# FFN activations: reciprocal rms, their combinations and a second copy of the high parts in PSUM; GpSimd splits none of the second half

## Chip, cores and metric

The kernel runs on one core of one Trainium2 chip. The metric is the device time of one execution in microseconds (us). TensorE (PE in the profile) multiplies, with weight loads shown as PEld; VectorE is DVE, ScalarE is ACT, GpSimd is POOL, and SyncE (SP) issues the DMAs. PSUM holds eight banks of 128 x 512 float32; SBUF holds all else on the core.

## What is computed

A hybrid decoder layer in float32 over 1024 tokens of width 1024: RWKV-7 time mixing beside dilated attention, then cross-attention to a memory, then the squared-ReLU MLP that the change is about, then a final norm. Cut to what matters:

```
D_MODEL = 1024; SEQ = 1024; FFN_DIM = 4096
def rmsnorm(x, g):
    return x * rsqrt(mean(x * x, axis=-1, keepdims=True) + 1e-6) * g
...
        h = h + memory_cross_attention(...)
        u = rmsnorm(h, norm_ffn_g[l]) @ ffn_w1[l]
        h = h + jnp.square(jax.nn.relu(u)) @ ffn_w2[l]
    return rmsnorm(h, norm_final_g)
```

## The kernel before

Activations lie transposed: `hT[d][half]` is a 128 x 512 tile of 128 channels (d = 0 to 7) by one half of the tokens. A float32 product is made of three matmuls on a high and a low part: `split(hi, lo, src)` rounds `src` to the high part with a ScalarE copy (line 128) and subtracts it from `src` for the low part (line 129), on VectorE or, where the caller says so, on GpSimd. PE then multiplies high by high, high by low and low by high (lines 1419 to 1421 in the MLP). Weights are split in the same way: ScalarE makes `wh` (line 1381), GpSimd `wl` (line 1382).

The MLP multiplies 2 x 2 blocks with seven block products in place of eight. Each of 16 up items (1024 x 256 of `ffn_w1`) and 16 down items (`ffn_w2`) runs seven products j = 0 to 6, each of 4 x 3 matmuls of 128 x 512 into one `ms` bank (`seventh`). Product j needs four split tiles `com[j]` of the activations and one split sum of weights. `up_evac` and `down_evac` take the products out of PSUM on VectorE; `up_evac` also makes the seven combinations of squared ReLUs and writes them to DRAM (`uscr`).

Where the activations come from:

- For the up items `first_coms(half)` makes them. `rms` turns the sums of squares into the reciprocal rms, spreads it over 128 x 512 by a matmul into PSUM (`pr`, from the pool `fps`), and copies it to SBUF (`rs`, line 1148). `normed` multiplies a tile of `hT` by its gain and by `rs` (line 1545). Half 0 gives `com[0]` and `com[1]`. Half 1 gives `com[3]`, `com[4]`, `com[2]`, `com[5]`, `com[6]` in that order, four tiles each: `normed`, an addition or subtraction (lines 1569, 1576, 1581, 1586), a split. Of its 20 splits GpSimd makes 12 low parts, VectorE 8.
- For the down items `second(g, j)` loads four tiles `ur` from `uscr` and splits them with VectorE. This is a *fill*: 28 tiles for each of four groups g of down items. Six SBUF buffers hold `ur` (tags `nt` four times, `rs`, `ssq`), so a load waits on SP's queue until an earlier tile has been split.

The first three up items run j = 0 and 1 early (`prologue`), while half 1 is being made; then item 0 runs j = 3, 4, 2, and products 5 and 6 after it, so it asks for all five groups of half 1 within a few products. After that the item order is 0, (5 of the item before), 1, (6 of the item before), 2, 3, 4. In a fill the same order asks for 28 tiles in eleven products.

What sets the order on each engine: the code is written in the order above, and a scheduler at build time orders each engine's instructions by its own estimate of times, within what the data and the buffers allow. On the chip each engine then runs its list strictly in that order. `acc_tile` gives one of two PSUM banks (`pacc`, two buffers) which the products before the MLP use; the MLP doesn't touch them.

Of the kernel before, what the change touches and what calls it, by code (L numbers as in the profile page):

```python
# [9 lines left out]
F32 = mybir.dt.float32  # L10
F32R = mybir.dt.float32r
AF = mybir.ActivationFunctionType
ALU = mybir.AluOpType
# [4 lines left out]
P = 128  # L18
D = 1024
S = 1024  # L20
H2 = 512
# [20 lines left out]
def hybrid_layer(ctx, tc, x, mem, norm_mix_g, w_in, shift_mu, w0, w2, a0, a2, g2, k_k, k_a, r_k, gn_w, gn_b,  # L42
                 p_rwkv, p_attn, w_out, norm_x_g, norm_mem_g, xa_wq, xa_wkv, xa_wo, norm_ffn_g, ffn_w1, ffn_w2,
                 norm_final_g, out):
    nc = tc.nc
# [4 lines left out]
    def nm(s):  # L50
        cnt[0] += 1
        return f"{s}_{cnt[0]}"
# [71 lines left out]
    def mm(ps, lhsT, rhs, start=True, stop=True):  # L124
        return nc.tensor.matmul(ps, lhsT, rhs, start=start, stop=stop)  # L125

    def split(hi, lo, src, lo_eng=None):
        nc.scalar.copy(hi, src)  # L128
        (lo_eng or nc.vector).tensor_tensor(lo, src, hi.bitcast(F32), op=ALU.subtract)  # L129
# [43 lines left out]
    def acc_tile():  # L173
        return pacc.tile([P, H2], F32, tag="acc", name=nm("acc"))
# [955 lines left out]
            nc.scalar.activation(sq, h, AF.Square)  # L1130
            nc.vector.tensor_tensor(ssq, ssq, sq, op=ALU.add)

    def rms(ssq, got, ps_tile):

        ps = ps_tile()
        for j in range(4):
            mm(ps[:, j:j + 1], ssq[:, j * P:(j + 1) * P], ones[:, 0:1])
        rt = bt.tile([P, 4], F32, tag="rt", name=nm("rt"), bufs=2)
        nc.scalar.activation(rt, ps[:, 0:4], AF.Sqrt, bias=eps_n, scale=1.0 / D)
        nc.vector.reciprocal(rt, rt)  # L1140
        rs = bt.tile([P, H2], F32, tag="rs", name=nm("rs"), bufs=1)
        for j in range(4):
            nc.vector.tensor_scalar_mul(rs[:, j * P:(j + 1) * P], ident, rt[:, j:j + 1])
        yield
        pr = ps_tile()
        for j in range(4):
            mm(pr[:, j * P:(j + 1) * P], ones, rs[:, j * P:(j + 1) * P])
        nc.scalar.copy(rs, pr)
        got.append(rs)
        yield  # L1150

    def norm_gen(ssq, res, half, gcol, ring):
        got = []
        yield from rms(ssq, got, ms_tile)
        rs = got[0]
        for d in range(NK):
            t = bt.tile([P, H2], F32, tag="nt", name=nm("nt"))
            nc.vector.scalar_tensor_tensor(t, hT[d][half], vec[:, gcol + d:gcol + d + 1], rs, op0=ALU.mult,
                                           op1=ALU.mult)
            ph = act_pair(ring)  # L1160
            split(ph[0], ph[1], t, nc.gpsimd if d % 2 else nc.vector)
            res.append(ph)
            yield
# [48 lines left out]
    ssqs, n1 = [None, None], [[], []]  # L1212
# [145 lines left out]
    fps = ctx.enter_context(tc.tile_pool(name="fps", bufs=2, space=PSUM, reuse_waits="tile"))  # L1358
    rings["U"] = fs
    RING = "BBACCAU"  # L1360
    com = [None] * 7

    def staged():
        return fs.tile([P, H2], F32, tag="sg", name=nm("sg"), bufs=7)

    def com_tiles(j):
        if RING[j] == "U":
            return [tuple(fs.tile([P, H2], F32R, tag=t, name=nm("u"), bufs=4) for t in ("uh", "ul")) for _ in range(4)]
        return [act_pair(RING[j]) for _ in range(4)]
# [155 lines left out]
    def down_views(g, q):  # L1525
        v = ffn_w2[0][g * D:(g + 1) * D, :].rearrange("(k h r) c -> h r k c", h=2, r=P)
        return [v[h, :, :, (2 * q + e) * P:(2 * q + e + 1) * P] for e in range(2) for h in range(2)]

    def second(g, j):

        com[j] = com_tiles(j)
        for i, ph in enumerate(com[j]):
            t = bt.tile([P, H2], F32, tag=UR[un[0] % 6], name=nm("ur"), bufs=4 if UR[un[0] % 6] == "nt" else 1)
            un[0] += 1
            r0 = ((g * 4 + i) * 7 + j) * P
            nc.sync.dma_start(t, uscr[r0:r0 + P, :])
            split(*ph, t, nc.vector)

    def first_coms(half):

        got = []
        yield from rms(ssqs[half], got, lambda: fps.tile([P, H2], F32, tag="f", name=nm("fm")))

        def normed(t, d):
            nc.vector.scalar_tensor_tensor(t, hT[d][half], vec[:, V_GFFN + d:V_GFFN + d + 1], got[0], op0=ALU.mult,
                                           op1=ALU.mult)

        if half == 0:
            for e in range(2):
                com[e] = com_tiles(e)  # L1550
                made.append(e)
                for i in range(4):
                    t = fs.tile([P, H2], F32, tag=("uh", "ul")[e], name=nm("b"), bufs=4)
                    normed(t, i + 4 * e)
                    split(*com[e][i], t, nc.gpsimd if i % 2 else nc.vector)
                    if e:

                        nc.vector.tensor_tensor(t, t, b0[0][i], op=ALU.subtract)
                    b0[e].append(t)
                    yield  # L1560
            return
        for j in range(2, 6):
            com[j] = com_tiles(j)
        b12 = []
        for i in range(4):
            b12.append(staged())
            normed(b12[i], i)
            t = staged()
            nc.vector.tensor_tensor(t, b12[i], b0[0][i], op=ALU.subtract)
            split(*com[3][i], t, nc.vector if i == 2 else nc.gpsimd)  # L1570
            yield
        made.append(3)
        for i in range(4):
            t = staged()
            normed(t, i + 4)
            nc.vector.tensor_tensor(b12[i], t, b12[i], op=ALU.subtract)
            split(*com[4][i], b12[i], nc.vector if i == 2 else nc.gpsimd)
            yield
        made.append(4)
        for i in range(4):  # L1580
            nc.vector.tensor_tensor(b0[0][i], b12[i], b0[0][i], op=ALU.add)
            split(*com[2][i], b0[0][i], nc.gpsimd if i % 2 else nc.vector)
            yield
        made.append(2)
        for i in range(4):
            nc.vector.tensor_tensor(b0[1][i], b0[1][i], b12[i], op=ALU.subtract)
            split(*com[5][i], b0[1][i], nc.gpsimd if i % 2 else nc.vector)
            yield
        made.append(5)
        com[6] = com_tiles(6)  # L1590
        for i in range(4):
            b22 = staged()
            normed(b22, i + 4)
            split(*com[6][i], b22, nc.gpsimd if i % 2 else nc.vector)
            yield
        made.append(6)

    UR, un = ("nt", "nt", "rs", "nt", "nt", "ssq"), [0]
    b0, made = [[], []], []

    def run(it, j):
        if it.get("fill"):
            second(it["fill"][0], j)
        while j not in made:
            next(coms, None)
        yield from seventh(it["st"], j, it["w"](j))
        it["st"].setdefault("seen", []).append(j)
        it["evac"](it["st"], j)
        yield
# [10 lines left out]
    def prologue():  # L1620
        for p in range(PRO):
# [3 lines left out]
            yield from run(it, 1)  # L1625

    weave((xout(o1, 1), 64, 0, 100), (first_coms(0), 10, 0, 80))

    def finish(d, half):
# [48 lines left out]
    def stream():  # L1678
        prev, ready = None, []
        for it, whole in items():  # L1680
# [22 lines left out]
            prev = it  # L1703

    coms = first_coms(1)
    weave((chain(prologue(), stream()), 48, 0, 100), (coms, 22, 0, 90))
_INS = ['x', 'mem', 'norm_mix_g', 'w_in', 'shift_mu', 'w0', 'w2', 'a0', 'a2', 'g2', 'k_k', 'k_a', 'r_k', 'gn_w', 'gn_b',
# [20 lines left out]
```

## Time and profile before

| what | us |
|---|---|
| median of 3 runs | 2441.41 (2440.43 to 2444.42) |
| the profiled execution, its own time | 2439.77 |
| its span, first to last instruction | 2438.1 |
| PE busy in the span | 2304.0 (95%) |
| VectorE busy | 1589.6 (65%) |
| ScalarE busy | 1046.3 (43%) |
| GpSimd busy | 922.5 (38%) |
| mean granted TensorE clock | 0.983 |

The MLP takes the span from 1723 us (the first matmul of line 1419) to its end at 2438 us. To read a stretch, compare its count of matmuls with that of a stretch where PE never waits: PE's busy time covers overlapping matmuls and is no measure by itself. A granted clock of 1.00 is 2.4 GHz, the lower of the two levels is 1.2 GHz.

### The profile page before, as it was taken

What the parts mean: (1) busy time and instruction counts of PE and PEld (TensorE: products, weight loads), DVE (VectorE), ACT (ScalarE), POOL (GpSimd) and SP (SyncE); (2) the same over time, 40 slices, a digit from 0 to 9 for tenths busy, and PEclk for the clock granted to TensorE, in tenths of its full rate; (3) what the DMA queues carried; (4) which work ended last, traced back from release to release, by engine and by line L of the source; (5) the groups of instructions that cost most, each with busy time, mean ns of one, the idle gap of its engine ahead of it and who ended that gap; (6) DMA issues with size and microseconds to landing.
All of it is one profiled execution on the core that took longest, in us unless ns stands there. A gap on an engine that the chain in (4) does not pass through costs nothing. (4 is left out here: it accounts for less than half of the span.)

```text
span 2438.1 us, 46897 instructions
## 1 busy us (share of the span) xinstructions
PE 2304.0 (95%) x18645; PEld 1834.2 (75%) x18645; DVE 1589.6 (65%) x2723; ACT 1046.3 (43%) x2032; POOL 922.5 (38%) x749
## 2 busy tenths in 40 slices
PE   6999999999999999999999999999889999899997
PEld 5777777777777777777678888887668887677775
DVE  6638677686786612232555664456799999797785
ACT  5525645645456434334433454444422223344344
POOL 4321222222222222111245535324555554565664
PEclk9999999999999999999999999999999999999998
DMA  4221111111111123121355553223244445554342
GB/s 171 57 64 34 37 39 34 37 43 34 37 33 33 49 70 102 40 69 41 90 176 157 163 153 115 68 60 91 65 143 156 151 155 178 160 168 124 114 133 75
DMA packets 301618, 226.73 MB, mean 93 GB/s; under 512 B 16229, under 2 KB 252375, under 8 KB 301399
## 3 DMA queue, kind: packets, MB, share of 16 engines
q1 hardware_dynamic: 301111, 223.20, 30.2%
q8 instruction: 147, 2.41, 0.4%
q14 instruction: 72, 0.59, 0.1%
q10 hardware_dynamic: 288, 0.52, 0.1%
HBM read 169.99 MB, written 53.67 MB: 92 GB/s over the span
## 5 line engine op out<-in xcount | busy, mean ns | idle before, releaser
L143 PE MATMUL acc<-ah,wh 128*128 128x512 f32 (+1 forms) x1600 | 652.2, 408 | 11.3 <-DVE h L1048 3.0
L144 PE MATMUL acc<-al,wh 128*128 128x512 f32 (+1 forms) x1600 | 618.3, 386 | 3.2 <-POOL al L231 1.9
L145 PE MATMUL acc<-ah,wl 128*128 128x512 f32 (+1 forms) x1600 | 618.1, 386 | 0.4 <-POOL wl L112 0.4
L112 POOL TENSOR_TENSOR wl<-wr,wh 128x512 fp32r<-128x512 f32 x248 | 334.5, 1350 | 708.5 <-ACT wh L110 665.5
L143 PEld LDWEIGHTS acc<-ah,wh 128*128 128x128 f32 x1600 | 302.9, 189 | 79.3 <-issue 4.9
L145 PEld LDWEIGHTS acc<-ah,wl 128*128 128x128 f32 x1600 | 302.6, 189 | 62.4 <-POOL wl L112 0.8
L144 PEld LDWEIGHTS acc<-al,wh 128*128 128x128 f32 x1600 | 303.3, 190 | 51.2 <-POOL al L231 3.5
L1419 PE MATMUL ms<-ah,wh 128*128 128x512 f32 x768 | 308.8, 402 | 18.2 <-DVE sg L1429 12.4
L1420 PE MATMUL ms<-al,wh 128*128 128x512 f32 x768 | 308.6, 402 | 15.6 <-DVE al L129 10.3
L1421 PE MATMUL ms<-ah,wl 128*128 128x512 f32 x768 | 306.8, 400 | 1.0 <-POOL wl L1382 0.9
L110 ACT CAST wh<-wr 128x512 fp32r<-128x512 f32 (+1 forms) x296 | 179.5, 607 | 297.7 <-PE acc L144 183.8
L1382 POOL TENSOR_TENSOR wl<-ws,wh 128x512 fp32r<-128x512 f32 x128 | 185.2, 1450 | 155.9 <-ACT wh L1381 148.3
L1419 PEld LDWEIGHTS ms<-ah,wh 128*128 128x128 f32 x768 | 147.4, 192 | 56.0 <-ACT wh L1381 6.8
L1420 PEld LDWEIGHTS ms<-al,wh 128*128 128x128 f32 x768 | 147.6, 192 | 54.6 <-DVE al L129 16.0
L1382 POOL TENSOR_TENSOR wl<-sr,wh 128x512 fp32r<-128x512 f32 x96 | 141.6, 1476 | 119.8 <-ACT wh L1381 119.6
L1421 PEld LDWEIGHTS ms<-ah,wl 128*128 128x128 f32 x768 | 147.7, 192 | 35.0 <-POOL wl L1382 2.8
L1381 ACT CAST wh<-ws 128x512 fp32r<-128x512 f32 x128 | 79.2, 620 | 203.5 <-PE ms L1420 162.9
L1381 ACT CAST wh<-sr 128x512 fp32r<-128x512 f32 x96 | 59.2, 620 | 137.8 <-PE ms L1420 122.2
L937 DVE CUSTOM_DVE_ANT_0 sS<-pS,bias 128x128 f32<-128x128 f32 (+1 forms) x96 | 30.2, 349 | 114.6 <-PE pS L125 114.4
L129 DVE TENSOR_TENSOR al<-ur,ah 128x512 fp32r<-128x512 f32 x96 | 93.7, 1014 | 0.4 <-ACT ah L128 0.4
L128 ACT CAST ah<-ur 128x512 fp32r<-128x512 f32 x96 | 58.5, 620 | 61.2 <-DMA ur<-uscr 54.7
L942 ACT ACTIVATE sS<-sS,nm 128x128 f32<-128x128 f32 (+1 forms) x96 | 42.5, 443 | 75.1 <-DVE nm L940 72.0
(414 smaller groups left out, 3982.4 us busy)
## 6 DMA issues: line engine op xcount, KB each, us to landing
sr<-in_ffn_w_dram SPq DMA_DIRECT2D x134, 256.0 KB
wr<-in_w_in_dram SPq DMA_DIRECT2D x120, 256.0 KB
ur<-uscr SPq DMA_DIRECT2D x112, 256.0 KB
uscr<-sg SPq DMA_DIRECT2D x93, 256.0 KB
gtscr<-gt SPq DMA_DIRECT2D x32, 256.0 KB
g<-gtscr SPq DMA_DIRECT2D x32, 256.0 KB
wr<-in_p_rwkv_dram SPq DMA_DIRECT2D x32, 256.0 KB
wr<-in_w_out_dram SPq DMA_DIRECT2D x32, 256.0 KB
```

The costliest lines, as they stand in the source:

```text
L110: nc.scalar.copy(h, raw)
L112: lo_eng.tensor_tensor(l, raw, h.bitcast(F32), op=ALU.subtract)
L128: nc.scalar.copy(hi, src)
L129: (lo_eng or nc.vector).tensor_tensor(lo, src, hi.bitcast(F32), op=ALU.subtract)
L143: mms.append(nc.tensor.matmul(ps, h, ah, start=(k == 0), stop=False))
L144: mms.append(nc.tensor.matmul(ps, h, al, start=False, stop=False))
L145: mms.append(nc.tensor.matmul(ps, l, ah, start=False, stop=(k == len(acts) - 1)))
L1381: nc.scalar.copy(h, raw)
L1382: nc.gpsimd.tensor_tensor(l, raw, h.bitcast(F32), op=ALU.subtract)
L1419: nc.tensor.matmul(ps, h[:, k, :], ah, start=(k == 0), stop=False)
L1420: nc.tensor.matmul(ps, h[:, k, :], al, start=False, stop=False)
L1421: nc.tensor.matmul(ps, l[:, k, :], ah, start=False, stop=(k == 3))
```

## The change

`rms` gets a flag: with it the spread reciprocal rms stays in its PSUM bank, and `normed` reads it there. The combinations of half 1 go into PSUM tiles (`acc_tile`) in place of SBUF tiles where a split follows directly, so the split's source is in PSUM. Where the source is in SBUF, a new `split_psum` is used (for `com[4]`, and for three of the four tiles of every `second`): ScalarE copies the high part a second time, into a PSUM tile, and VectorE subtracts that copy from the source. GpSimd makes no low parts of half 1 any more; half 0 keeps its division between VectorE and GpSimd.

```
-    def rms(ssq, got, ps_tile):
+    def rms(ssq, got, ps_tile, keep=False):
...
-        nc.scalar.copy(rs, pr)
-        got.append(rs)
+        if keep:
+            got.append(pr)
+        else:
+            nc.scalar.copy(rs, pr)
+            got.append(rs)
...
+    def split_psum(hi, lo, src):
+
+        nc.scalar.copy(hi, src)
+        t = acc_tile()
+        nc.scalar.copy(t, hi.bitcast(F32))
+        nc.vector.tensor_tensor(lo, src, t, op=ALU.subtract)
...
     def second(g, j):
...
-            split(*ph, t, nc.vector)
+            (split if i == 3 else split_psum)(*ph, t)
...
-        yield from rms(ssqs[half], got, lambda: fps.tile([P, H2], F32, tag="f", name=nm("fm")))
+        yield from rms(ssqs[half], got, lambda: fps.tile([P, H2], F32, tag="f", name=nm("fm")), True)
...
             normed(b12[i], i)
-            t = staged()
+            t = acc_tile()
             nc.vector.tensor_tensor(t, b12[i], b0[0][i], op=ALU.subtract)
-            split(*com[3][i], t, nc.vector if i == 2 else nc.gpsimd)
+            split(*com[3][i], t)
...
-            t = staged()
+            t = acc_tile()
             normed(t, i + 4)
             nc.vector.tensor_tensor(b12[i], t, b12[i], op=ALU.subtract)
-            split(*com[4][i], b12[i], nc.vector if i == 2 else nc.gpsimd)
+            split_psum(*com[4][i], b12[i])
...
-            nc.vector.tensor_tensor(b0[0][i], b12[i], b0[0][i], op=ALU.add)
-            split(*com[2][i], b0[0][i], nc.gpsimd if i % 2 else nc.vector)
+            t = acc_tile()
+            nc.vector.tensor_tensor(t, b12[i], b0[0][i], op=ALU.add)
+            split(*com[2][i], t)
...
-            nc.vector.tensor_tensor(b0[1][i], b0[1][i], b12[i], op=ALU.subtract)
-            split(*com[5][i], b0[1][i], nc.gpsimd if i % 2 else nc.vector)
+            t = acc_tile()
+            nc.vector.tensor_tensor(t, b0[1][i], b12[i], op=ALU.subtract)
+            split(*com[5][i], t)
...
-            b22 = staged()
+            b22 = acc_tile()
             normed(b22, i + 4)
-            split(*com[6][i], b22, nc.gpsimd if i % 2 else nc.vector)
+            split(*com[6][i], b22)
```

The order on the engines changes with it. VectorE at the start of half 1, before: the first combinations (`sg` from `b`), with one split among them (`al_18812`), since GpSimd has the others.

```order
L1545 SCALAR_TENSOR_TENSOR sg_18831<-h_1_11283,vec,rs_18767 128x512
L1404 TENSOR_TENSOR ws_19025<-sr_18985,sr_18989 128x512
L1569 TENSOR_TENSOR sg_18833<-sg_18831,b_18444 128x512
L1545 SCALAR_TENSOR_TENSOR sg_18843<-h_1_11285,vec,rs_18767 128x512
L1429 TENSOR_TENSOR ua_18852<-ua_18787,ms_18795 128x512
L1569 TENSOR_TENSOR sg_18845<-sg_18843,b_18480 128x512
L1545 SCALAR_TENSOR_TENSOR sg_18867<-h_1_11287,vec,rs_18767 128x512
L1569 TENSOR_TENSOR sg_18869<-sg_18867,b_18499 128x512
L1545 SCALAR_TENSOR_TENSOR sg_18879<-h_1_11289,vec,rs_18767 128x512
L1569 TENSOR_TENSOR sg_18881<-sg_18879,b_18535 128x512
L129 TENSOR_TENSOR al_18812<-sg_18869,ah_18811 128x512
```

The same place on VectorE now; `fm` is the spread reciprocal rms in PSUM, `acc` a combination in PSUM. Lines are those of the changed kernel (1555 was 1545, 1579 was 1569, 1432 was 1429, 1402 was 1399).

```order
L1555 SCALAR_TENSOR_TENSOR sg_18829<-h_1_11283,vec,fm_18777 128x512
L1555 SCALAR_TENSOR_TENSOR sg_18841<-h_1_11285,vec,fm_18777 128x512
L1579 TENSOR_TENSOR acc_18831<-sg_18829,b_18443 128x512
L1579 TENSOR_TENSOR acc_18843<-sg_18841,b_18479 128x512
L1432 TENSOR_TENSOR ua_18850<-ua_18785,ms_18793 128x512
L129 TENSOR_TENSOR al_18806<-acc_18831,ah_18805 128x512
L129 TENSOR_TENSOR al_18808<-acc_18843,ah_18807 128x512
L1555 SCALAR_TENSOR_TENSOR sg_18865<-h_1_11287,vec,fm_18777 128x512
L1555 SCALAR_TENSOR_TENSOR sg_18877<-h_1_11289,vec,fm_18777 128x512
L1579 TENSOR_TENSOR acc_18867<-sg_18865,b_18498 128x512
L1579 TENSOR_TENSOR acc_18879<-sg_18877,b_18534 128x512
L1402 TENSOR_TENSOR ws_19002<-ws_19001,sr_18993 128x512
```

The tiles come in pairs, as many as there are `acc` banks, and every low part is now VectorE's own, two places behind the combination it belongs to.

ScalarE in the first fill, before: high parts of activations (`ah` from `ur`) between those of weights (`wh`); `sg` from `ms` is the first step of a down product's evacuation.

```order
L128 CAST ah_21581<-ur_21589 128x512
L128 CAST ah_21583<-ur_21593 128x512
L128 CAST ah_21653<-ur_21661 128x512
L1381 CAST wh_21605<-sr_21511 128x512
L128 CAST ah_21585<-ur_21597 128x512
L1381 CAST wh_21623<-ws_21487 128x512
L128 CAST ah_21587<-ur_21601 128x512
L1381 CAST wh_21681<-ws_21678 128x512
L1500 COPY sg_21558<-ms_21545 128x512
```

The same place on ScalarE now (line 1534 is the high part in `split_psum`, 1536 its copy to PSUM, 1384 was 1381, 1503 was 1500).

```order
L1534 CAST ah_21601<-ur_21609 128x512
L1534 CAST ah_21603<-ur_21615 128x512
L1536 COPY acc_21612<-ah_21601 128x512
L1536 COPY acc_21618<-ah_21603 128x512
L1384 CAST wh_21631<-sr_21525 128x512
L1534 CAST ah_21679<-ur_21687 128x512
L1384 CAST wh_21649<-ws_21501 128x512
L1534 CAST ah_21605<-ur_21621 128x512
L1536 COPY acc_21624<-ah_21605 128x512
L1503 COPY sg_21578<-ms_21565 128x512
```

Two copies to PSUM stand behind a pair of high parts and ahead of the next `wh`; a third copy stands ahead of the evacuation `sg`, and it needs a bank that VectorE has finished with.

## Rows read from the trace of the kernel before

**Rows 1.** Windows: stretch, its length, busy us (instructions) by engine, clock, DMA share, GB/s

```profile
1729.40:1778.60 49.20, 35.99 (x118) 24.41 (x118) 48.97 (x55) 20.76 (x36) 29.76 (x19) 0.82 0.22 70
1800.00:1830.00 30.00, 26.16 (x112) 20.62 (x111) 26.31 (x32) 7.18 (x12) 16.26 (x11) 1.00 0.47 156
1900.00:1950.00 50.00, 50.00 (x218) 40.78 (x217) 46.85 (x51) 12.65 (x21) 26.24 (x19) 1.00 0.46 151
2049.00:2106.00 57.00, 48.01 (x177) 35.51 (x175) 56.32 (x68) 25.79 (x46) 22.43 (x16) 0.88 0.73 227
2140.00:2180.00 40.00, 36.75 (x157) 28.91 (x156) 40.00 (x49) 20.96 (x38) 21.43 (x14) 1.00 0.73 224
2220.00:2268.00 48.00, 44.20 (x185) 35.21 (x184) 47.41 (x55) 25.04 (x45) 25.10 (x18) 0.96 0.64 198
2310.00:2351.00 41.00, 37.33 (x152) 29.98 (x151) 40.97 (x49) 21.13 (x37) 20.38 (x14) 0.92 0.65 199
```

**Rows 2.** Waits of PE, 1735 to 1815 us: total us, times, longest us

```profile
PE ms L1420 <- POOL al L129: 5.2, 4, 2.4
PE ms L1420 <- DVE al L129: 4.2, 3, 3.1
```

**Rows 3.** Waits of PE, 2040 to 2420 us

```profile
PE ms L1419 <- DVE sg L1429: 9.8, 4, 3.7
PE ms L1420 <- DVE al L129: 6.1, 3, 4.0
```

**Rows 4.** Durations by line: ns least/median/most, first and last start us, shapes

```profile
L129 DVE TENSOR_TENSOR al<-ur,ah x96: 676/680/1809, 2050.8 to 2343.0; 128x512 fp32r<-128x512 f32 x96
L1429 DVE TENSOR_TENSOR sg<-sg,ms x70: 672/680/689, 1764.3 to 2410.1; 128x512 f32<-128x512 f32 x70
L1545 DVE SCALAR_TENSOR_TENSOR sg<-h,vec,rs x12: 739/1087/1790, 1730.8 to 1775.6; 128x512 f32<-128x512 f32 x12
L228 DVE SCALAR_TENSOR_TENSOR tm<-pt,vec,rsb x16: 734/745/751, 15.8 to 44.2; 128x512 f32<-128x512 f32 x16
```

**Rows 5.** Timeline of VectorE, with one GpSimd row: start us, duration us

```profile
1729.43 0.68 DVE L1398 TENSOR_TENSOR ws<-sr,sr 128x512 f32<-128x512 f32 x1
...
1776.83 0.68 DVE L129 TENSOR_TENSOR u<-sg,u 128x512 fp32r<-128x512 f32 x1
...
1782.51 0.68 DVE L1429 TENSOR_TENSOR sg<-sg,ms 128x512 f32<-128x512 f32 x1
...
1783.71 1.74 POOL L1382 TENSOR_TENSOR wl<-sr,wh 128x512 fp32r<-128x512 f32 x1
...
1784.33 1.67 DVE L1485 TENSOR_TENSOR sg<-sg,sg 128x512 f32<-128x512 f32 x1
...
1787.63 0.68 DVE L1487 TENSOR_TENSOR sg<-sg,sg 128x512 f32<-128x512 f32 x1
1788.23 0.68 DVE L1488 TENSOR_TENSOR sg<-ua,sg 128x512 f32<-128x512 f32 x1
```

**Rows 6.** GpSimd's groups, 1729 to 1780 us: busy us, mean ns, idle before

```profile
L129 POOL TENSOR_TENSOR al<-sg,ah 128x512 fp32r<-128x512 f32 x6 | 9.8, 1638 | 3.2 <-ACT ah L128 3.2
```

**Rows 7.** VectorE's splits by shape, 1500 to 2438 us and 2138 to 2360 us

```profile
L129 DVE TENSOR_TENSOR al<-ur,ah 128x512 fp32r<-128x512 f32 x96 | 93.7, 1014 | 0.4 <-ACT ah L128 0.4
...
L129 DVE TENSOR_TENSOR al<-ur,ah 128x512 fp32r<-128x512 f32 x72 | 71.6, 1035 | 0.0
```

**Rows 8.** ScalarE's copies by line: ns least/median/most

```profile
L128 ACT CAST ah<-ur x96: 612/620/626, 2050.1 to 2339.7; 128x512 fp32r<-128x512 f32 x96
L1439 ACT COPY ua<-ms x16: 566/581/584, 1728.0 to 2042.5; 128x512 f32<-128x512 f32 x16
L267 ACT COPY f<-acc x24: 579/1068/1100, 918.8 to 1187.7; 128x512 f32<-128x512 f32 x24
```

**Rows 9.** Waits of SP's queue, 2120 to 2360 us, and of ScalarE, 2040 to 2360 us

```profile
SPq L1536 <- DVE al L129: 66.5, 69, 3.3
ACT ah L128 <- DMA ur<-uscr: 54.7, 35, 4.8
```

## The prediction, made before the changed kernel ran

> **What bounds the kernel now.** I read the table of windows first, then PE's waits in the stretches it singled out, then VectorE's durations and its timeline there. Between 1900 and 1950 us PE is never idle and starts 218 matmuls in 50 us, one every 0.229 us [rows 1]. That is the measure. In the other windows I count what is missing against it: 214.5 places and 118 matmuls from 1729.4 to 1778.6 us, so 22.1 us lost; 4.3 us lost from 1800 to 1830; 16.4 us in the first fill (2049 to 2106); 4.0, 5.6 and 6.1 us in the other three fills. Together 58.5 us, 32.1 of it in the fills. In each of these windows but the second VectorE is busy at least 98% of the time, and the reader should see that this holds nowhere for ScalarE (42 to 52%) or GpSimd (39 to 60%) [rows 1]. PE's waits name VectorE's work too: low parts `al`, and products that VectorE has not yet taken out of PSUM (`sg`, line 1429), 9.8 and 6.1 us in the fills [rows 3]. At half 1 GpSimd's low parts hold PE up as much as VectorE's (5.2 and 4.2 us [rows 2]). So the stretches are bound by VectorE's list, and the rest of the MLP by PE.
>
> VectorE's list is slow for one reason that the durations show. A subtraction with both sources in SBUF takes 0.68 us or up to 1.81 us; with a source in PSUM it takes 0.67 to 0.69 us, all 70 times [rows 4]. The timeline shows when: with GpSimd in an operation of 1.74 us, VectorE's line 1485 on two SBUF tiles takes 1.67 us, while line 1429 with a PSUM source takes 0.68 us [rows 5]. In a queue without waits two operations start 0.60 us apart [rows 5]; I cost each at that, and a held one at what it had.
>
> **Reciprocal rms in PSUM.** `normed` (line 1545) took 0.74 to 1.79 us, median 1.09; with one PSUM source the same form took 0.73 to 0.75 us [rows 4]. One ScalarE copy of 0.58 us [rows 8] goes ahead of the first `normed` in each half; in half 1 VectorE has weight sums to do in that time, so I count nothing. In half 0 the faster `normed` lies beside PE's cross-attention products: nothing.
>
> **Half 1.** Before, VectorE works without a gap from 1729.43 to the end of the last split at 1777.51 us [rows 5]: 48.1 us for 53 operations, 10 of which have a PSUM source. The other 43 so took 48.1 - 10 x 0.60 = 42.1 us, 0.98 each. In the new order 68 operations stand up to the same point: 12 low parts come from GpSimd, and three weight sums of the next item have moved ahead. Of the 68, 46 read PSUM: 46 x 0.60 = 27.6 us. The other 22 cost between 0.60 (never held) and 0.98 each, 13.2 to 21.6 us, so 40.8 to 49.2 us in all. I take the share of GpSimd that is left: its 12 splits at 1.64 us [rows 6] are about 20 of its 30 busy us [rows 1], a third stays, and 0.38 x 1/3 gives 0.73 each, 16.1 us. Sum 43.7 us. The added wait is VectorE's own: it stands until ScalarE has made the high part, and in `com[4]` the copy too. What stands between in the list (one to three operations) covers one copy of 0.62 us; for the second tile of `com[4]` two copies are 1.2 us against one operation of 0.60, and `com[6]` is short by some 0.3 us. With hand-over I put 1.3 us, behind which the next combinations queue. So 45.0 in place of 48.1 us: PE gets the last group **3.1 us** earlier. The three weight sums that are done early (2.2 us) are off the backlog that costs 4.3 us around 1800 to 1830; I count 1.0 us. Ends: 0 from the slow end (49.2 + 1.3 against 48.1, less the sums) and 8 us.
>
> **The fills.** 21 of each 28 tiles change. VectorE's share falls from a mean of 1.035 us in the last three fills, and (93.7 - 71.6) / 24 = 0.92 us in the first [rows 7], to 0.68. Counting only the 18 tiles with 96 `al` rows: 18 x 0.355 = 6.4 us less of VectorE in a later fill, 18 x 0.24 = 4.3 us in the first. In the first, PE loses 16.4 us and VectorE is the only busy engine, so nearly all should arrive: 0.8 x 4.3 = **3.4 us**. In the later fills VectorE saves more than PE loses (15.7 us in all), so something else comes last next. That is ScalarE's list: 21 more copies of 0.58 us are 12.2 us a fill, on top of 21.0, 25.0 and 21.1 us [rows 1], so 33.2, 37.2 and 33.3 us in stretches that would be 36.0, 42.4 and 34.9 us long if PE lost nothing. It fits, without room for waits. I count 60% of the 15.7: **9.4 us**. No row shows ScalarE or VectorE writing PSUM. The nearest for ScalarE are 0.57 us (reading PSUM) and 0.63 us (SBUF to SBUF), the farthest copy of this size 1.10 us [rows 8]; I take 0.58, the contiguous one. At 1.10 the 12.2 us become 23, and the fill falls to the slower rival. For VectorE I take the 0.68 us that both kinds of source show; 0.1 us more on the 20 combinations that go to PSUM would be 2 us.
>
> The Trainium skill ("Perfetto Trace Analysis", Optimizing Scalar/DVE Operations) speaks against this: VectorE's access overhead is about 125 ns on PSUM and 60 ns on SBUF. By it some 130 operations would each cost 65 ns more, an estimate of 8.5 us by that page. The 0.680 us median of both kinds [rows 4] doesn't bear it out for reads, and the sum above goes by the rows.
>
> **The sum.** 3.1 + 1.0 + 3.4 + 9.4 = 16.9 us. Against the profiled execution, 2439.77 us (span 2438.1 and 1.7 us around it), that is 2422.9; the median of the runs lies 1.6 us above it, so **2424 us**, 0.7% less than 2441.41. Its own range is 2415 to 2433: 40 to 80% of the later fills, and half 1 from 0 to 8 us.
>
> **Rivals.**
>
> *All of it comes back.* VectorE never meets GpSimd in half 1 (8 us), the later fills lose nothing (15.7 us), the first gives 4.3 us: 28 us, 2413 us, and less if the clock stays up: it is 0.82 in half 1 and 0.88 in the first fill [rows 1], after PE had stood still. For it: VectorE is at 98% and more. Against: ScalarE's list above has 1.6 to 5.2 us of room in a later fill. 14%.
>
> *The ring of `ur` sets the fills.* SP waits 69 times for a low part before it may load the next tile, 66.5 us, and ScalarE 35 times for a tile to land, 54.7 us [rows 9]. If the way round (load, high part, low part, free buffer) is what paces a fill, a copy of 0.58 us more on it takes away the 0.35 us that the subtraction gives, and only half 1 gains: 2441.4 - 4.1 = 2437 us. Against: VectorE had no gap in these stretches, so the tiles were there before it was. 17%. The case that the copy simply costs ScalarE what VectorE saves ends here too.
>
> *ScalarE becomes the bound: slower.* A copy needs one of two banks that VectorE must first have read, and behind it in ScalarE's list stand the next high part, `wh` for PE and the evacuation `sg`. With a mean wait w of each copy, a later fill needs 33.2 + 21 w, 37.2 + 21 w and 33.3 + 21 w us on ScalarE; it decides above w = 0.32, 0.51 and 0.37 us, where these reach today's 40, 48 and 41 us. At w = 0.7 us the three are 7.9, 3.9 and 7.0 us longer, the first fill and half 1 still give 7.5 us: +11, 2452 us. For it: waits of that size are common, VectorE's held operations take 1.1 us longer. Against: most copies are made ahead of VectorE's turn, and the held operations get rarer. 14%.
>
> **How the numbers follow.** Forecast 55%, all of it 14%, ring 17%, slower 14%. About 0.2%, 5 us, is what a measurement of this kernel can tell from no change: faster means under 2436.5, slower over 2446.3. Forecast and the first rival are faster, and a sixth of the ring's 17% too: 0.72. The rest of the ring is the same: 0.14. Slower 0.14. The range runs from 2408 (past the first rival, for the clock) to 2444 (past the ring, short of the slower case), which leaves out 14% above and a few in a hundred below.
>
> **What would show it.** Right: low parts `al` from `acc` at 0.67 to 0.69 us with no held ones; matmuls from 1729 to 1778 us up from 118 towards 135; in the later fills 5 to 15 more matmuls in 40 us; ScalarE at 75 to 90% there, GpSimd's `wl` nearer 1.3 us. Wrong: VectorE idle before `al` for ScalarE's copy, the copy waiting for VectorE's `al` for over 0.4 us at a time, `wh` late for PE, copies into PSUM well above 0.63 us; or VectorE with gaps while SP waits as long as before for the ring.

## The result, and the profile after

The changed kernel takes 2404.24 us (median of 4 runs, 2404.06 to 2407.52) against 2440.92 us (2439.53 to 2444.42) for the kernel before on the same chip: a ratio of 0.9856, interval 0.9842 to 0.9869, or 36.7 us. The forecast was 2424 with a range of 2408 to 2444, so the sign was right, the gain is more than twice the 16.9 us of the sum, and the time lies 4 us below the range. The profiled execution is the slowest of the four, 2407.52 us (span 2405.8, granted clock 0.989).

In the lines below, 1419 to 1421 have become 1422 to 1424, 1382 is 1385, 1429 is 1432, 1426 is 1429, 1338 is 1341, 1545 is 1555; the subtraction of `split_psum` is line 1537, its second copy line 1536.

Windows of the kernel after (columns as in [rows 1]); the places are those of [rows 1], earlier by about what had been gained up to there:

```profile
1725.60:1770.00 44.40, 36.75 (x134) 25.92 (x135) 43.24 (x70) 23.92 (x42) 13.12 (x11) 0.92 0.28 89
1790.00:1820.00 30.00, 30.00 (x133) 24.66 (x132) 28.02 (x33) 7.81 (x13) 15.81 (x12) 1.00 0.51 167
1882.00:1932.00 50.00, 50.00 (x219) 40.82 (x218) 46.02 (x52) 12.17 (x20) 26.37 (x18) 1.00 0.45 149
2036.00:2093.00 57.00, 48.67 (x196) 35.68 (x195) 47.29 (x69) 37.21 (x68) 27.10 (x19) 1.00 0.75 240
2121.00:2161.00 40.00, 38.92 (x168) 31.09 (x167) 34.33 (x51) 33.11 (x61) 22.03 (x16) 1.00 0.72 226
2198.00:2246.00 48.00, 45.45 (x197) 36.14 (x195) 40.53 (x59) 35.93 (x67) 29.03 (x21) 1.00 0.63 199
2280.00:2321.00 41.00, 41.00 (x179) 33.45 (x179) 37.43 (x54) 34.66 (x65) 24.69 (x18) 1.00 0.67 206
```

Count PE's matmuls first. In half 1 there are 134 in 44.4 us where there were 118 in 49.2; the stretch behind it has 133 in 30 us where there were 112; the fills have 196, 168, 197 and 179 where there were 177, 157, 185 and 152 [rows 1]. PE's pace where nothing is late is unchanged (219 in 50 us). VectorE, at 98% or more in all of the fills before, is at 83 to 91% now, and ScalarE has risen to 65 to 85%.

Durations in the kernel after (ns least/median/most, first and last start):

```profile
L1537 DVE TENSOR_TENSOR al<-ur,acc x72: 672/675/689, 2040.3 to 2315.2; 128x512 fp32r<-128x512 f32 x72
L1536 ACT COPY acc<-ah x76: 576/588/593, 1739.1 to 2314.2; 128x512 f32<-128x512 f32 x76
L1555 DVE SCALAR_TENSOR_TENSOR acc<-h,vec,fm x8: 742/750/756, 1736.1 to 1766.9; 128x512 f32<-128x512 f32 x8
L1385 POOL TENSOR_TENSOR wl<-ws,wh x128: 1273/1297/1842, 1731.9 to 2374.3; 128x512 fp32r<-128x512 f32 x128
```

None of the 72 changed subtractions is held: the largest is 689 ns where [rows 4] has 1809. What PE still waits for, 2026 to 2390 us (total, times, longest), is short; the answering rows of before are [rows 3]:

```profile
PE ms L1423 <- DVE al L1537: 4.1, 5, 1.3
PE ms L1422 <- DVE h L1432: 3.9, 3, 2.2
PE ms L1423 <- DVE al L129: 3.3, 5, 1.3
PE ms L1422 <- DVE sg L1432: 1.4, 2, 0.9
```

**Where the time went.** Five instants of each trace cut the program into parts: VectorE's first `rs<-ident` of half 0 (1680.13 us before) and of half 1 (1727.58), ScalarE's copy of the eighth up item (`ua<-ms`, 1887.92), and its copies of the fourth and of the last down item (`sg<-ms`, 2137.52 and 2394.97). A part's gain is its length before less its length in the other kernel, each from one profiled execution. The first column, everything ahead of half 0, is the same code in all of them, so it is chance, and it is large; the other columns don't contain it, but that of half 1 has a chance of its own, the clock (see e12).

```
gain against before, us      ahead  half 0  half 1  1st fill  later fills
the changed kernel             1.3     2.5     9.5       5.8         13.2
e13_same (the same kernel)     3.0     2.5    11.1       7.5         13.8
e1_rms                        -4.8     2.5     5.3      -0.7          0.5
e2_half1                       2.2     2.5    11.1       0.6          1.4
e3_fills                      -2.7     0.0    -0.1       5.8         14.1
e4_unread                      0.9     2.5     6.0       3.4          0.1
e5_half1_dve                   0.6     0.0     5.8      -0.5         -0.5
e6_half0_sbuf                -12.1     0.0     6.8       7.1         14.5
e7_twice                       0.7     2.5    11.1      -1.9         11.4
e8_all4                        0.1     2.5     9.5       6.8         19.1
e10_banks                      1.9     2.5    11.0       6.7         14.6
e12_half1_sbuf                 4.9     2.5     3.2       6.3         14.7
e14_all4_banks                 0.0     2.6     9.5       2.6         21.9
the forecast                     -       0     4.1       3.4          9.4
```

The theory going into the experiments was that VectorE's list sets the pace, and that a source in PSUM shortens it because such an operation is never held while GpSimd works; the rivals were the ones of the prediction and, for half 1, that GpSimd's own slow splits were the cost. The medians of before beside the experiments were 2441.14 (e1 to e4), 2440.81 (e5 to e8) and 2439.78 us (the rest).

### The profile page after: what moved, and what is told of

It reads as the page before. It is cut to its first block, busy times and chain, and to the rows that moved or that the text cites. A ratio compares the mean times of both kernels' runs of the same rounds, so it can differ in the third digit from the quotient of the medians.

```text
span 2405.8 us, 47020 instructions
## 1 busy us (share of the span) xinstructions
PE 2292.9 (95%) x18645; PEld 1827.2 (76%) x18645; DVE 1545.9 (64%) x2735; ACT 1088.3 (45%) x2118; POOL 889.4 (37%) x737
## 5 line engine op out<-in xcount | busy, mean ns | idle before, releaser
L1385 POOL TENSOR_TENSOR wl<-ws,wh 128x512 fp32r<-128x512 f32 x128 | 178.6, 1398 | 177.7 <-ACT wh L1384 149.6
L399 ACT ACTIVATE gt<-acc 128x512 f32<-128x512 f32 x32 | 19.0, 594 | 127.1 <-PE acc L145 121.3
L1432 DVE TENSOR_TENSOR sg<-sg,ms 128x512 f32<-128x512 f32 x70 | 47.7, 683 | 37.5 <-PE ms L1424 36.6
```

The source lines that it names most:

```text
L1385: nc.gpsimd.tensor_tensor(l, raw, h.bitcast(F32), op=ALU.subtract)
L1432: (eng or nc.vector).tensor_tensor(dst, a, b, op=ALU.add)
```

## The experiments

**e1_rms: only the reciprocal rms in PSUM.**

```
-        nc.scalar.copy(rs, pr)
-        got.append(rs)
+        got.append(pr)        # both halves; all else as before
```

> Only the first part of the change, on the kernel before: the spread reciprocal rms stays in PSUM for both halves; combinations, splits and fills as before. Theory (VectorE's list is what PE waits for, held operations are what makes it long): half 0 gives the 2.5 us that the trace of the changed kernel shows there, and in half 1 the 12 operations of line 1545 lose 12 x (1.23 - 0.74) = 5.9 us of VectorE, so 2441 - 2.5 - 3 to 6 = 2433 to 2436 us. Rival (the first part is hidden beside other work, as the prediction had it): 2440 to 2442 us.

Measured: 2434.38 us, ratio 0.9982 (0.9964 to 1.0000); the time alone can't tell it from no change. The parts can: 2.5 us in half 0 and 5.3 in half 1, and nothing in the fills (-0.7 and 0.5). `normed` is 736 ns in the median in half 1 where [rows 4] has 1087.

**e2_half1 and e3_fills: the change cut in two.** e2 has half 0 and half 1 as changed and the fills as before; e3 has only the fills.

```
-            split(*ph, t, nc.vector)
+            (split if i == 3 else split_psum)(*ph, t)      # e3: this alone; e2: all but this
```

> The changed kernel without its change of the fills: reciprocal rms and half 1 as changed, every tile of the down items split from SBUF as before. Theory (the parts add up, each in its own stretch): half 0 and half 1 give 2.5 + 9.5 us, so about 2429 us, with the four fills as long as before. Rival (what half 1 gains is given back behind it, or the fills gain from another order alone): under 2420 or above 2436 us.

> The other piece: the kernel before with the second copy in PSUM for three of four tiles of each fill, first and second half as before. Theory: 19 us (the fills of the profile) to 23 us (with what the undisturbed runs show on top), so 2418 to 2422 us. Rival (the fills gain only because half 1 leaves less backlog): above 2430 us.

Measured: 2428.04 us, ratio 0.9943 (0.9921 to 0.9964), and 2420.68 us, ratio 0.9909 (0.9893 to 0.9925): 13.1 and 20.5 us, together 33.6 of the 36.7. The parts show that they don't touch each other: the fills give 19.9 us with half 1 unchanged (19.0 and 21.3 with it changed), and the two halves give 13.6 us with the fills unchanged (12.0 and 13.6). The forecast had 12.8 and 4.1: the larger miss is in the halves.

**e4_unread: the copies are made, but nobody reads them.**

```
-        nc.vector.tensor_tensor(lo, src, t, op=ALU.subtract)
+        nc.vector.tensor_tensor(lo, src, hi.bitcast(F32), op=ALU.subtract)
```

> The changed kernel, but VectorE subtracts the high part in SBUF as before; ScalarE still makes each copy in PSUM, which nothing reads. ScalarE's work and the order are near those of the changed kernel, only the source of the subtraction differs. Theory (a PSUM source is what counts, since it is not held by GpSimd): 88 subtractions cost again 0.3 to 0.4 us more, so most of the fills' gain is lost, and what ScalarE's copies cost shows on top: 2422 to 2432 us. Rival (the gain of the fills comes from another order, or from GpSimd's lighter work): 2404 to 2410 us.

Measured: 2427.58 us, ratio 0.9948 (0.9929 to 0.9967). ScalarE does the same work as in the changed kernel, only VectorE's second source is in SBUF again. VectorE's group in the fills of e4 (busy us, mean ns, idle before):

```profile
L1537 DVE TENSOR_TENSOR al<-ur,ah 128x512 fp32r<-128x512 f32 x72 | 69.1, 992 | 0.0
```

and of the changed kernel:

```profile
L1537 DVE TENSOR_TENSOR al<-ur,acc 128x512 fp32r<-128x512 f32 x72 | 47.8, 678 | 8.5 <-ACT acc L1536 8.5
```

69.1 us against 47.8, and the fills keep 3.5 us of the 19.0. That settles the mechanism of the fills: it is where VectorE reads, not a new order. (The four subtractions of `com[4]` read SBUF again too, and half 1 gains 6.0 us; e12 comes back to that.)

**e5_half1_dve: GpSimd splits none of half 1, but nothing moves to PSUM.**

```
-            split(*com[3][i], t, nc.vector if i == 2 else nc.gpsimd)
+            split(*com[3][i], t)        # and so for com[4], com[2], com[5], com[6]; else as before
```

> The kernel before with one thing changed: in half 1 all low parts of the combinations are VectorE's, with both sources in SBUF as before; nothing reads PSUM that did not. Theory (it is the PSUM source that makes the changed half 1 pay, and the hand-over of GpSimd's splits to VectorE only pays with it): VectorE's list of half 1 grows from 53 to about 68 operations, some 58 of them on SBUF, and each of these is held as often as GpSimd works; between 0.68 and 0.98 us each the list takes 45 to 63 us in place of 48.1, so no gain: 2439 to 2452 us. Rival (it is GpSimd's slow splits of 1.64 us that the matmuls waited for, whatever VectorE reads): half 1 gains most of the 13 us that e2 gained, 2429 to 2434 us, and the medians of VectorE's durations there fall without any PSUM source.

Measured: 2436.92 us, ratio 0.9984 (0.9973 to 0.9994); half 1 gains 5.8 us. Neither theory had this. I had expected 45 to 63 us for VectorE's longer list; it is at the short end. It runs from 1728.80 to 1773.69 us, 44.9 us for 65 operations, against 48.1 us for 53 before and 44.4 for 68 after, although nothing more than before reads PSUM. Nor does the rival's size fit, 5.8 of 13. GpSimd is busy 10.5 of 43.3 us there, so there is little left to be held by:

```profile
1728.70:1772.00 43.30, 34.27 (x115) 23.14 (x115) 43.18 (x64) 19.75 (x35) 10.54 (x7) 0.83 0.21 66
```

**e12_half1_sbuf: the changed kernel, with half 1's combinations in SBUF.**

```
-            t = acc_tile()
+            t = staged()                 # com[2] to com[6]; com[4] by split, not split_psum
```

> The changed kernel, but half 1's combinations stay in SBUF: GpSimd still splits none of them and `normed` still reads the reciprocal rms in PSUM, but all 20 low parts of half 1 have both sources in SBUF. e5 showed that VectorE's list of half 1 needs 44.8 us without any PSUM source when GpSimd splits nothing, against 44.4 us in the changed kernel. Theory (in half 1 it is GpSimd's silence that pays, PSUM as a source adds little where nobody holds the port): 0 to 3 us slower than the changed kernel, 2404 to 2407.5 us. Rival (the combinations in PSUM carry what e5 lacked, 4 us of the 9.5 us): 4 to 7 us slower, 2408 to 2411 us.

Measured: 2416.86 us (2408.12 to 2421.02), ratio 0.9905 (0.9879 to 0.9931). Half 1 gains 3.2 us where the changed kernel gains 9.5 and 11.1: the rival had the direction, by the medians the loss is larger than its 4 to 7 us, and what I had concluded from e5 fell. VectorE's list takes 45.9 us here (1721.99 to 1767.90). The order of size is odd, though. The last low part of half 1 comes 1.5 us later than in the changed kernel (measured below), yet the part is 6 to 8 us longer. The windows show where that is lost. First 89 us from 1 us after `rs<-ident`, then the 12 us from 38 us after it; in turn before, e12, after:

```profile
1728.58:1817.58 89.00, 72.68 (x272) 53.32 (x271) 85.91 (x95) 30.25 (x52) 55.31 (x34) 0.88 0.34 108
1765.58:1777.58 12.00, 7.27 (x16) 3.63 (x16) 12.00 (x17) 4.28 (x7) 5.89 (x4) 0.72 0.22 68
```

```profile
1721.14:1810.14 89.00, 78.01 (x286) 57.12 (x285) 84.95 (x111) 30.77 (x52) 37.21 (x24) 0.87 0.36 115
1758.14:1770.14 12.00, 9.59 (x20) 5.70 (x19) 11.21 (x19) 4.63 (x8) 2.66 (x1) 0.50 0.18 66
```

```profile
1724.79:1813.79 89.00, 77.46 (x306) 58.68 (x305) 85.80 (x117) 33.52 (x58) 34.33 (x25) 0.94 0.39 125
1761.79:1773.79 12.00, 10.63 (x45) 8.34 (x46) 11.46 (x17) 4.73 (x8) 4.65 (x4) 1.00 0.27 87
```

In those 12 us PE is busy 9.6 us in e12 and 10.6 in the changed kernel, but at a granted clock of 0.50 against 1.00, with 20 matmuls against 45. 25 matmuls at 0.229 us are 5.7 us, most of the difference. e5 is like e12:

```profile
1764.95:1776.95 12.00, 9.94 (x21) 6.02 (x21) 11.21 (x19) 4.75 (x8) 3.67 (x2) 0.50 0.32 102
```

e1 has 0.53 and 23 matmuls; e2, e7, e8, e10, e13 and e14 all have 1.00 and 45. e6, whose half 1 is the changed one too, has 0.86 and 38 there, and gains 6.8 us where they gain 9.5 to 11.1. 0.50 is the lower level, 1.2 GHz. The same 89 and 12 us of e6, then the 12 us of e4:

```profile
1740.70:1829.70 89.00, 78.22 (x294) 59.06 (x294) 83.20 (x115) 32.55 (x57) 32.77 (x24) 0.88 0.37 118
1777.70:1789.70 12.00, 10.64 (x38) 8.24 (x39) 9.90 (x16) 4.10 (x7) 3.45 (x3) 0.86 0.18 61
```

```profile
1762.20:1774.20 12.00, 9.30 (x38) 7.06 (x39) 11.46 (x19) 4.98 (x9) 2.56 (x2) 1.00 0.12 45
```

Two things follow that the totals hide. The changed half 1, with the same code in eight kernels, gains 6.8 us at a granted clock of 0.88 over the 89 us (e6), 9.5 at 0.92 and 0.94 (e8, e14 and the changed kernel), and 11.0 to 11.1 at 0.96 and 0.98 (e7, e10, e2, e13): one execution of half 1 is good to some 4 us only. And e4 gets its last low part 48.8 us after `rs<-ident`, 1.0 us later than e12, but has 1.00 and 38 matmuls in the 12 us and gains 6.0 us against 3.2. A later feed with the fuller clock gained more than an earlier one without it.

**e6_half0_sbuf: the changed kernel, with half 0's reciprocal rms in SBUF.**

```
-        yield from rms(ssqs[half], got, lambda: ..., True)
+        yield from rms(ssqs[half], got, lambda: ..., half == 1)
```

> The changed kernel, but half 0 takes its reciprocal rms from SBUF as before; half 1 and the fills stay changed. The prediction had counted half 0 at nothing, the marks of the two traces show about 2.5 us there. Theory (the held `normed` of half 0 stood ahead of the evacuation of the cross-attention products, and PE waited for it): 2 to 4 us slower than the changed kernel, 2406 to 2408.5 us, with the last evacuation of the cross-attention about 2.5 us later. Rival (half 0 lies beside PE's work and the 2.5 us are a difference between two executions): within 0.5 us of the changed kernel, 2404 to 2405 us.

Measured: 2412.86 us (2406.37 to 2423.47), ratio 0.9875 (0.9854 to 0.9897). That median is no price of half 0: the profiled execution, the slowest, lies 12.1 us behind before already ahead of half 0. The part itself is sharp. From `rs<-ident` of half 0 to that of half 1 it is 47.40 to 47.45 us in the four kernels with the reciprocal rms of half 0 in SBUF (before, e3, e5, e6), and 44.89 to 44.95 us in all ten with it in PSUM. So 2.5 us, theory right.

**e7_twice: every second copy of the fills made twice.**

```
         nc.scalar.copy(t, hi.bitcast(F32))
+        if twice:
+            nc.scalar.copy(t, hi.bitcast(F32))
```

> The changed kernel, but ScalarE makes each second copy of the fills twice into the same bank: 72 more copies of 0.588 us, 42 us more of ScalarE, about 10.6 us a fill. It measures how far ScalarE is from being the bound. By the rows of the changed kernel ScalarE is busy 61 to 73% of a fill of 50 to 60 us, so 80 to 92% with the copies. Theory (ScalarE has room, VectorE or PE still ends last): 0 to 8 us slower than the changed kernel, 2404 to 2412 us. Rival (ScalarE's list is nearly what ends last, as the prediction's slower case had it): most of the fills' gain of about 20 us goes, 2418 to 2430 us, and VectorE waits for `acc` of the second copy for more than 20 us in place of 8.5.

Measured: 2416.46 us, ratio 0.9899 (0.9885 to 0.9914). It falls between the two: 49 us more of ScalarE (72 copies for `al` and 12 for `u`, which the expectation left out) cost 12.2 us against the changed kernel's median. VectorE waits 13.2 us for the copy, not over 20:

```profile
DVE al L1539 <- ACT acc L1538: 13.2, 16, 2.9
```

The first fill loses 1.9 us against before; the later ones keep 11.4 of 13.2. The first fill in e7:

```profile
2036.00:2093.00 57.00, 46.35 (x172) 33.78 (x171) 45.93 (x65) 45.73 (x86) 20.55 (x15) 0.91 0.67 217
```

One copy leaves ScalarE room. With two, the first fill is slower than before although ScalarE is busy in 45.73 of 57 us only, 80%, less than in the last fill of the changed kernel, where PE lost nothing. So the busy share doesn't say when this list is full. The copy made twice also holds its bank longer, and the clock was 0.91; which of these cost the first fill was not tried.

**e8_all4, e10_banks, e14_all4_banks: further on the same way.** e8 splits the fourth tile through PSUM too; e10 sends the second tile's copy to the two banks that held the reciprocal rms; e14 does both.

```
-            (split if i == 3 else split_psum)(*ph, t)
+            split_psum(*ph, t)                                     # e8
+            split(*ph, t) if i == 3 else split_psum(*ph, t, i == 1)   # e10: True takes t from fps, tag "f"
+            split_psum(*ph, t, i % 2 == 1)                         # e14
```

> The changed kernel, but the fourth tile of each group of a fill is also split through the second copy in PSUM (96 low parts in place of 72). VectorE saves 24 x (0.969 - 0.678) = 7 us in all, ScalarE gets 24 x 0.588 = 14 us more. Theory (VectorE's list still ends last in the fills): 2 to 5 us faster than the changed kernel, 2399 to 2402 us. Rival (PE or the two banks end last by now): 0 to 6 us slower, 2404 to 2410 us, with more waits of the copies for VectorE's `al` than the 5.3 us of the changed kernel.

> The changed kernel, but the second copy of the second tile of each group of a fill goes to the two banks that held the reciprocal rms, so copies and VectorE's subtractions alternate over more banks. In the changed kernel the copies wait 5.3 us for VectorE's `al`, and VectorE 8.5 us for the copy, 12 times. Theory (two banks couple ScalarE and VectorE, and the coupling still costs PE): 1 to 4 us faster than the changed kernel, 2400 to 2403 us, with less than 2 us of waits of the copies for `al`. Rival (these waits lie off the path): within 1 us, 2403 to 2405 us.

> The changed kernel with all four tiles of a fill's group split through a copy in PSUM, the second and fourth in the two banks that held the reciprocal rms. e8 alone gave -1.5 us in the medians, with 11.1 us of waits of the copies for `al` and 14.2 us of VectorE for the copies. Theory (the last 24 held subtractions cost 7 us of VectorE, and with four banks the waits go): 3 to 6 us faster than the changed kernel, 2398 to 2401 us. Rival (PE is the bound by now in the fills): within 1.5 us of e8, 2401 to 2404 us.

> The changed kernel itself, word for word, once more beside the others of this call. It says how much of the difference to it is chance, and whether the dip of the clock in the third fill of its profile (0.85 from 2240 to 2250 us) comes back. Expected: 2404 to 2407.5 us, no dip in most executions.

Measured, the last three beside each other: e13 2405.43 us, ratio 0.9853 (0.9832 to 0.9874); e10 2404.13 us, 0.9847 (0.9827 to 0.9867); e14 2402.60 us, 0.9834 (0.9812 to 0.9857); and e8, run beside e5 to e7, 2402.78 us, 0.9851 (0.9832 to 0.9870). The intervals overlap: none is shown to be faster than the changed kernel. In e10 the copies' waits for `al` fall from 5.3 us to

```profile
ACT acc L1536 <- DVE al L1537: 0.3, 1, 0.3
```

and the time stays: the two banks are off the path. In the later fills e8 and e14 gain 19.1 and 21.9 us where the changed kernel has 13.2 and 13.8, the direction of e8's theory, but the medians show only 1.5 and 2.8 us of it, and e14's first fill gains 2.6 us only where the changed kernel's two executions have 5.8 and 7.5. e13 has no dip of the clock in its third fill, and its later fills gain 13.8 us, so that dip in the profile of the changed kernel (0.85 from 2240 to 2250 us) was that execution's.

## Why the prediction was half right

The mechanism of the sum held; its terms were too small. Half 0 was put at 0 and gave 2.5 us, half 1 with its backlog at 4.1 and gave 9.5, the first fill at 3.4 and gave 5.8, the later fills at 9.4 and gave 13.2. So the parts of the profiled pair add up to 31.0 us where the sum had 16.9, and the medians, 36.7 us apart, put the time below the range's lower end, 2408.

**What bounds the kernel: right.** VectorE's list is what the stretches waited for, and in the fills the place of its second source is the reason (e4). The signs named for it came: no held `al` from `acc`, 134 matmuls in half 1, 10 to 26 more in 40 us of a later fill, `wl` at 1.30 us (the 26 is more than the 5 to 15 named).

**Half 0 at nothing: wrong by 2.5 us.** The step said that the faster `normed` "lies beside PE's cross-attention products". It stands ahead of their evacuation in VectorE's list. VectorE in half 0 before:

```profile
1686.08 1.78 DVE L1545 SCALAR_TENSOR_TENSOR b<-h,vec,rs 128x512 f32<-128x512 f32 x1
1687.79 1.78 DVE L129 TENSOR_TENSOR al<-b,ah 128x512 fp32r<-128x512 f32 x1
1689.49 1.78 DVE L1545 SCALAR_TENSOR_TENSOR b<-h,vec,rs 128x512 f32<-128x512 f32 x1
1691.19 0.68 DVE L1338 TENSOR_TENSOR h<-acc,h 128x512 f32<-128x512 f32 x1
```

and PE's waits of before, 1680 to 1720 us:

```profile
PE acc L143 <- DVE h L1338: 2.0, 2, 1.5
```

This wait is most of the missing term. The evacuation `h<-acc,h` starts 11.1 us after `rs<-ident` (1680.13) there, and 8.0 us after it (1678.86) in the changed kernel:

```profile
1686.85 0.68 DVE L1341 TENSOR_TENSOR h<-acc,h 128x512 f32<-128x512 f32 x1
```

After, PE is busy 40.0 us of the same 40. Here, then, work beside PE was not free, because something that PE waited for was queued behind it on the same engine.

**Half 1, 3.1 us: VectorE's list was right, its end was not.** I forecast 45.0 us for the list; it took 44.4 (1725.64 to 1770.02), with the 68 operations and the 46 that read PSUM of the sum. e5 shows that the reason given is only one of two that give about this length: with GpSimd's splits gone the operations are seldom held even from SBUF (6 of 65 took over 0.8 us, where 15 of 53 had). What failed is the end of the comparison. VectorE's last split was not the last low part before; GpSimd's was. In the timeline of before, VectorE's start of half 1 and GpSimd's last split:

```profile
1727.58 1.93 DVE L1143 TENSOR_SCALAR rs<-ident,rt 128x128 f32<-128x128 f32 x4
...
1777.09 1.55 POOL L129 TENSOR_TENSOR u<-sg,u 128x512 fp32r<-128x512 f32 x1 [2.00 <-ACT u L128]
```

The same two instants after:

```profile
1723.79 1.93 DVE L1143 TENSOR_SCALAR rs<-ident,rt 128x128 f32<-128x128 f32 x4
...
1769.33 0.69 DVE L129 TENSOR_TENSOR u<-acc,u 128x512 fp32r<-128x512 f32 x1 [0.36 <-ACT u L128]
```

1778.64 - 1727.58 = 51.1 us before, 1770.02 - 1723.79 = 46.2 after: 4.8 us (unrounded), not 3.1. (e12: 1767.90 - 1720.14 = 47.8; e5: 46.7; e4: 48.8; e6, with the changed half 1: 47.8.) I took the end of the stretch from the engine whose list I was summing up, though GpSimd's slower splits [rows 6] were part of the same group.

**The backlog, 1.0 us: too small.** Behind half 1 PE lost 4.3 us before [rows 1]; now it has 133 matmuls in 30 us and loses none. And TensorE's granted clock, which the prediction left to the first rival, is part of half 1's gain: 45 matmuls at 1.00 in 12 us where e12 has 20 at 0.50. Feed, backlog and clock lie in one another here: the last low part 4.8 us sooner and 9.5 to 11.1 us gained with the clock at 1.00; 3.3 sooner and 3.2 gained at 0.50 (e12); 4.4 sooner and 5.8 gained at 0.50 (e5); 2.3 sooner and 6.0 gained at 1.00 (e4). No run held the clock still. The nearest to it is e6: 0.88 over the 89 us, as before, and 6.8 us gained. As an estimate from that one execution, feed and backlog are worth some 7 us where the sum had 4.1, and the fuller clock of the other executions 3 to 4 us more. What sets the clock in this stretch stays open.

**The fills: the mechanism right, both discounts wrong.** First fill: 3.4 forecast, 5.8 and 7.5 measured. I had counted only what 18 subtractions save, 4.3 us, and 0.8 of that. The 4.3 was itself read low: 93.7 and 71.6 us in [rows 7] are busy times, in which overlapping operations count once; by the means a subtraction of the first fill took 0.95 us, not 0.92, and the 18 save 4.9. But VectorE needs 47.29 us for 69 operations where it needed 56.32 for 68 [rows 1], 9 us less: other operations with two sources in SBUF were held less often too. `sg<-sg` (now line 1429) in the first fill before, 2049 to 2106 us, and after, 2036 to 2093 us:

```profile
L1426 DVE SCALAR_TENSOR_TENSOR sg<-sg 128x512 f32<-128x512 f32 x3 | 4.3, 1426 | 0.0
```

```profile
L1429 DVE SCALAR_TENSOR_TENSOR sg<-sg 128x512 f32<-128x512 f32 x3 | 2.2, 724 | 0.0
```

Why these meet GpSimd less often was not tried by itself. Later fills: 9.4 forecast, 13.2 and 13.8 measured. I had cut PE's 15.7 us to 60% because the copies fit "without room for waits". ScalarE is busy 83, 75 and 85% there, as forecast (75 to 90%), but there was room: e7 doubles the added copies, and the later fills lose 1.8 of the 13.2. The rest that is lost by the windows is 1.5, 2.9 and 0 us (168, 197 and 179 matmuls at 0.229).

**The rivals.** The ring of `ur` fell: SP waits for low parts 22.6 + 21.9 us where it waited 66.5 [rows 9], and the fills gained most. ScalarE as the bound fell: of the kernels with copies in the fills only e7, with two a tile, has a first fill slower than before. "All of it comes back" (2413) was the nearest and had 14%; its half 1 of 8 us was close to 9.5. It lacked half 0's 2.5 us, and it named the fuller clock without a price; most of the rest of the way from 2413 to 2404 lies in no part of the table.

**The prices.** ScalarE's copy into PSUM was taken at 0.58 us and took 0.588. VectorE's writes to PSUM were taken at 0.68; `normed` into PSUM has a median of 750 ns and into SBUF 742 and 738, so some 10 ns more. By the Trainium skill ("Perfetto Trace Analysis", Optimizing Scalar/DVE Operations), VectorE's access overhead is about 65 ns more on PSUM than on SBUF. No row shows that: 675 ns with a PSUM source, 680 with both in SBUF and not held [rows 4].

**The sum.** 0 + 3.1 + 1.0 + 3.4 + 9.4 = 16.9 us forecast; 2.5 + 9.5 + 5.8 + 13.2 = 31.0 us in the profiled pair, and 34.9 with e13 in its place. The 1.3 and 3.0 us ahead of half 0 are chance, and the medians, 36.7 us apart, may contain such a share.

## What to carry to other kernels

Where one engine is busy without a gap and PE waits for it, what it saved arrived nearly whole here: cut such a saving only for a next engine that a run shows to be full. The busy share is no such sign: 85% cost nothing in the last fill, and 80% went with a loss in e7's first. Before costing a shorter operation at nothing, read what is queued behind it on its own engine; before costing a shorter list by its end, look for the last producer on every engine. A kernel whose two halves are changed separately shows the sum of both (33.6 of 36.7 us here), but whether parts inside one half add can't be read here: 5.3 us (e1) and 5.8 us (e5) alone and 3.2 together (e12) are one execution each, and half 1 alone varied by 4 us with the clock.

## What was unexpected about the hardware

- **The same list came with more than one clock, and its worth with it.** The changed half 1 gained 6.8 us where the granted clock was 0.88 over 89 us (e6) and 11.1 where it was 0.98 (e2, e13). In a stretch of 12 us PE was busy 9.6 to 10.6 us in all of these: 20 to 23 matmuls at a granted 0.50 to 0.53 (e1, e5, e12), or 45 at 1.00 (the changed kernel and the six that share its half 1 and show 1.00). In the changed kernel PE had been busy 1.94 and 1.24 of 3 us from 34 to 40 us after `rs<-ident` and 2.90 of the next 3, all at 1.00; in e12 2.05, 2.22 and 1.79 of the same 3 us, at 0.77, 0.50 and 0.50.
- **A silent GpSimd does nearly as much for VectorE as a PSUM source.** The list of half 1 took 44.9 us (e5, 65 operations) and 45.9 us (e12) from SBUF with GpSimd's splits gone, 44.4 from PSUM (68 operations). In the fills, where GpSimd keeps making `wl`, the place of the source decides: 992 ns against 678 (e4). The Trainium skill ("SBUF — State Buffer", Who interferes with whom) has the rule, that an instruction with two SBUF inputs contends with a GpSimd instruction that reads SBUF and one with at most one does not; both halves of it agree with these rows.
- **ScalarE is a little faster with one end in PSUM:** 588 ns for the copy `acc<-ah` into PSUM (76 times) and 586 for the cast `ah<-acc` out of it (line 128, 12 times), against 620 for the cast `ah<-ur` with both ends in SBUF [rows 8].
